# Context values times exponentials: two quarters in one product of 512 queries, at every second quarter of a neighbourhood-attention layer

## The chip, the cores and the metric

The kernel runs on one core of a Trainium2 chip. The metric is device time in microseconds (us) of one execution. Before the change the median of three runs is 630.89 us (629.98 to 631.63).

## The reference

One layer of a diffusion backbone: 1024 latent tokens on a grid of 16 x 64, 256 context tokens, 8 heads of 64. What matters here is the softmax that runs over a latent window and the whole context together:

```python
s_lat = jnp.einsum('biqhd,birkhd->bhiqrk', q_rot, k_rows) * scale + bias
s_lat = jnp.where(col_valid[:, None, :], s_lat, -jnp.inf)
s_ctx = jnp.einsum('biqhd,blhd->bhiql', q_plain, kc) * scale
p = jax.nn.softmax(jnp.concatenate([s_lat, s_ctx], axis=-1), axis=-1)
o = einsum('bhiqrk,birkhd->biqhd', p_lat, v_rows) + einsum('bhiql,blhd->biqhd', p_ctx, vc)
attn = o * jax.nn.silu(za)
conv = bg * conv3(cg * u) * jax.nn.silu(zc)
x_new = x + gate * (concatenate([attn, conv]) @ w_out)
```

Each of `q, k, v, za, u, bg, cg, zc` is a 512-column part of one input projection of the normalised, modulated tokens.

## The kernel before

All matrix products are made to float32 accuracy from parts in a rounded format: a tensor is split in a high part (a copy or an exponential by ScalarE, ACT in the rows) and the rest (a subtraction by VectorE, DVE). A product is then three matmuls on TensorE (PE): high x high, low x high, high x low. Names ending in `h` and `l` are these parts: `phc` and `plc` for the exponentials of the context, `phl` and `pll` for those of the latent window, `uh` and `ul` for projection weights.

The program has three stages. Up to some 275 us it normalises the tokens and projects q, k and v. From there to some 520 us it runs the attention, with the remaining projections (gates and convolution inputs) as filler between its matmuls. Then it makes the output projection.

The attention is a pipeline of 35 **quarters**, written out in order by `quarter(n)`; in this stage the order of every compute engine is fixed as written (`strict`), while the order of the DMA issues on SyncE (SP) is left to the scheduler. A quarter works on 256 queries (16 columns of the grid) of one head. In quarter n:

- the scores of unit n are made (`pss`, four matmuls), and the context scores of unit n+1 (`pc`, four matmuls; ScalarE copies half of it to `sc`);
- for unit e = n-2 the maximum per query is found: two transposes of the running maxima `mx` into `pmx`, called T in the prediction, a reduction `rm` on VectorE, and two transposes back (`back()`, `pmx<-ci,rm`) that spread the result over the partitions, copied by ScalarE to `mg`. VectorE then subtracts `mg` from `sc` and `sb`, and ScalarE takes the exponentials;
- unit o = n-3 is multiplied by V: `ctx_out` for the context (six matmuls of 65 output rows, 256 columns) and `lat_out` for the latent window, both added up in a bank of 512 queries, `po`.

VectorE's order in a quarter is: `rm`; `pll` of the unit before; up to three **chores** (work for the filler: splits `ul`, products of the convolution such as `cu<-pu,ub` and `cv<-pu,cv`); the subtractions of `mg`; the additions of the bias to `pss`, into `sb`; the maxima (`mx<-pc,sc`, then two `mx<-mx,sb`); `plc`. The next quarter's T reads `mx`.

The filler comes in **ticks** of six `pu` matmuls of 512 columns. `TICKS` gives each quarter's number, three in most, two in quarters 5 and 8, four in 17, 18, 27 and 28. A filler product of 24 matmuls fills one of two banks (tag `U`); the bank is free again when a copy or a chore has read it.

The lines of `quarter` that the change moves against each other are, in the order before:

```python
if live(o):
    heads[o // 4].ctx_out(o % 4)
do_dves(3)
if back and n > 2:
    back()
now = pair_of(n)
for i, hd_, j in now:
    hd_.scores(j, sbank[:, i])
for m in ctx_now:
    heads[m // 4].ctx_scores(m % 4)
if back and n == 2:
    back()
```

Of the kernel before, what the change touches and what calls it, by code (L numbers as in the profile page):

```python
# [19 lines left out]
P = 128  # L20
# [5 lines left out]
NB = 8  # L26
# [13 lines left out]
def body(tc, es, x, ctxt, w_ada, b_ada, w_in, q_g, k_g, rpbr, w_out, vecs, cst, out):  # L40
# [21 lines left out]
    pe, act, dve, pool = every = [ordered(e) for e in (nc.tensor, nc.scalar, nc.vector, nc.gpsimd)]  # L62
# [258 lines left out]
    def do_acts():  # L321
        for c in soon + (slow if not any(c[1] and c[1].__name__ == "product" for c in soon) else []):
            if c[0]:
                c[0]()
                c[0] = None

    def do_dves(most=99):
        while most > 0 and slow and slow[0][2] is not None and not slow[0][0]:
            slow.pop(0)[1]()
            most -= 1  # L330
        for queue in chores:
            while queue and not queue[0][0] and (queue is soon or most > 0 and not soon):
                on_dve = queue.pop(0)[1]
                if on_dve:
                    on_dve()
                    most -= 1
# [670 lines left out]
    class head:  # L1007
# [74 lines left out]
        def ctx_exp(self, g):  # L1082
            sc = self.cps[g]
            m = mg[:, g * 256:(g + 1) * 256].rearrange("p (o q) -> p o q", o=1)
            dve.tensor_tensor(sc, sc, m.broadcast_to([P, 2, 256]), ALU.subtract)
            ph = ap.tile([P, 2, 256], F32R, name="phc", tag="phc", bufs=1)
            pl = ap.tile([P, 2, 256], F32R, name="plc", tag="plc", bufs=1)
            act.activation(ph, sc, AF.Exp)
            act.activation(sc, sc, AF.Exp)
            self.cps[g] = ph, pl  # L1090
            return lambda: dve.tensor_tensor(pl, sc, ph[:].bitcast(F32), ALU.subtract)

        def ctx_out(self, g):
            ph, pl = self.cps.pop(g)
            for i in range(2):
                self.pv(g // 2, lambda o: o[:, (g % 2) * 256:(g % 2 + 1) * 256], NB + i, ph[:, i], pl[:, i], False)

        def finish(self, bank):

# [5 lines left out]
    def pair_of(n):  # L1105

        h, g = divmod(n, 4)
        return [(a, heads[h], 2 * g + a) for a in range(2)] if 0 <= h < NH else []

    def both(v, n, part=slice(0, 31)):  # L1110

        lo, hi = span(2 * (n % 4))
        return v[:, :, part.start * 12:min(part.stop, hi - lo) * 12]

    def maxima_of(n):

# [9 lines left out]
    def maxima(e):  # L1126

        blocks = turned(e) if e < 4 * NH else []
        nb = len(blocks)
        if not blocks:  # L1130
            return None
        pm = psm.tile([P, 512], F32, name="pmx", tag="C", bufs=2)
        for i, b in enumerate(blocks):
            pe.transpose(pm[:, i * P:(i + 1) * P], mx[:, b * P:(b + 1) * P], ident)
        rm = ap.tile([P, 2], F32, name="rm", tag="rm", bufs=8)
        dve.tensor_reduce(rm[:, :nb], pm[:, :nb * P].rearrange("p (i k) -> p i k", i=nb), AX.X, ALU.max)

        def back():
            for i in range(nb):
                pe.transpose(pm[:, 256 + i * P:256 + (i + 1) * P], rm[:, i:i + 1].broadcast_to([P, P]), ident)  # L1140
            v, step = mg[:, blocks[0] * P:], (blocks[-1] - blocks[0]) * P or P
            act.copy(bass.AP(v.tensor, v.offset, [list(v.ap)[0], [step, nb], [1, P]]),
                     pm[:, 256:256 + nb * P].rearrange("p (i k) -> p i k", i=nb))
        return back

    def quarter(n):

        live = lambda m: 0 <= m < 4 * NH
        ticks = TICKS[n]
        e, o = n - 2, n - 3
        back = maxima(e) if e >= 0 else None
        while lat_rest:
            lat_rest.pop()()
        if live(o):
            heads[o // 4].ctx_out(o % 4)
        do_dves(3)
        if gating and next(gating[0], "end"):  # L1160
            gating.pop(0)
        if back and n > 2:
            back()
        now = pair_of(n)
        for i, hd_, j in now:
            hd_.scores(j, sbank[:, i])
        if n == 0:
            next(fill)
            ticks -= 1
        ctx_now = [m for m in ([0, 1] if n == 0 else [n + 1]) if live(m)]  # L1170
        for m in ctx_now:
            heads[m // 4].ctx_scores(m % 4)
        if back and n == 2:
            back()
        if live(e):
            ctx_rest = heads[e // 4].ctx_exp(e % 4)
            sb = sbs.pop(e)
            w = both(sb, e)
            w4 = w.rearrange("p a (c r) -> p a c r", r=12)
            dve.tensor_tensor(w4, w4, maxima_of(e), ALU.subtract)  # L1180
            exps[e] = [ap.tile([P, 2, 384], F32R, name=m, tag=m, bufs=2) for m in ("phl", "pll")]
            ph, pl = (both(v, e) for v in exps[e])
            act.activation(ph, w, AF.Exp)
            act.activation(w, w, AF.Exp)
        for _ in range(n > 0):
            next(fill, None)
        done = []
        if o >= 0:
            pho, plo = exps.pop(o)
            for i, hd_, j in pair_of(o):  # L1190
                hd_.lat_out(j, pho[:, i], plo[:, i])
                if j in (5, 7):
                    done.append((hd_, j // 7))
                    if j == 7 and hd_.s:
                        ready.append(hd_.p)
        if now:
            sb = sbs[n] = sb_new()
            bt = now[0][1].bt[:].rearrange("p v n -> p (v n)")[:, :1128].rearrange("p (a n) -> p a n", a=2)
            for at, slot, w_ in (((0, 31, 8), (8, 15, 16)), ((0, 0, 31),), ((0, 0, 31),), ((0, 0, 15), (15, 39, 8)))[n % 4]:
                dve.tensor_tensor(sb[:, :, at * 12:(at + w_) * 12], sbank[:, :, at * 12:(at + w_) * 12],  # L1200
                                  bt[:, :, slot * 12:(slot + w_) * 12], ALU.add)
# [53 lines left out]
    for n in range(NT + 3):  # L1255
# [54 lines left out]
        if 1 < n <= NT + 1:  # L1310
            m, r = n - 2, (n - 2) % NB
# [69 lines left out]
    with sbuf("att") as ap, psum("psb") as psb:  # L1381
# [6 lines left out]
        for n in range(len(TICKS)):  # L1388
            h, g = divmod(n, 4)
            if 0 < h < NH and g == 0:  # L1390
                heads[h].load_v()
            if h + 1 < NH and g:
                nx = heads[h + 1]
                for load in ((nx.masks, nx.load_q), (nx.load_k,), ())[g - 1]:
                    load()
            quarter(n)
            if ready:
                p = ready.pop()
                if p < NPAIR - 1:
                    gating.append(gated(p))  # L1400
                else:
                    recip(p, ap)
# [146 lines left out]
```

## Time and profile before

| | before |
|---|---|
| median of three runs | 630.89 us (629.98 to 631.63) |
| the profiled execution | 630.4 us, of which the span of instructions is 628.6 us |
| TensorE busy | 621.7 us, 99% of the span |
| VectorE busy | 433.5 us, 69% |
| ScalarE busy | 326.5 us, 52% |
| granted TensorE clock | 0.999 of full speed |
| from 283.8 to 509.1 us | TensorE 225.13, VectorE 189.16, ScalarE 148.57 us busy of 225.30 |

A row of a timeline is: start in us, duration in us, engine, line, operation, output<-inputs, shapes, how many follow one another; in brackets the idle time of the engine before it and what ended that. Nearly all rows have line 55, since one helper records every operation, so that they are told apart by tile names. A row of the waits is: who waited, for whom, us in total, times, longest.

### The profile page before, as it was taken

The page shows a single profiled execution, that of the slowest core. Times are in us where ns is not written, and L with a number is a line of the kernel's source. Part 1 is how long each engine was busy: PE and PEld are TensorE (multiplying, and loading weights), DVE is VectorE, ACT ScalarE, POOL GpSimd, SP SyncE. Part 2 cuts the span into 40 slices and gives each one's busy share as a digit, 9 for nine tenths or more (in the row PEclk, how much of TensorE's full clock was granted, in tenths as well). Part 3 has the DMA queues.
Part 4 walks back from the last instruction along what each step waited for, and adds up shares of the span by engine and source line. Part 5 has one row for each costly group of instructions (what it writes and reads, how often), then busy time and mean ns, then how long its engine had stood idle before and what let it go on. Part 6 is the DMA issues. An engine that isn't in the chain of part 4 may idle for free.

```text
span 628.6 us, 10005 instructions
## 1 busy us (share of the span) xinstructions
PE 621.7 (99%) x3487; PEld 538.5 (86%) x3488; DVE 433.5 (69%) x889; ACT 326.5 (52%) x712; POOL 77.6 (12%) x102
## 2 busy tenths in 40 slices
PE   8999999999999999999999999999999999999998
PEld 3577899999999999888888888888888888888887
DVE  1887858866866855568897879988998865594111
ACT  3777835524625545346576568566774845450000
POOL 1305014113223221100000000000000002004200
PEclk9999999999999999999999999999999999999999
DMA  8983737967784995885474553775542235963621
GB/s 316 347 282 124 178 111 259 286 204 244 236 293 137 302 320 181 298 264 214 144 238 140 192 172 127 214 254 181 190 136 76 61 93 163 357 226 121 213 102 50
DMA packets 104030, 126.45 MB, mean 201 GB/s; under 512 B 10689, under 2 KB 70553, under 8 KB 102700
## 3 DMA queue, kind: packets, MB, share of 16 engines
q1 hardware_dynamic: 97516, 114.24, 55.3%
q10 hardware_dynamic: 6208, 11.05, 5.6%
q0 software_dynamic: 256, 0.54, 0.3%
q8 instruction: 27, 0.44, 0.3%
q14 instruction: 23, 0.19, 0.1%
HBM read 89.04 MB, written 39.04 MB: 204 GB/s over the span
## 4 chain that ended last, share of the span: by engine, by line
PE 96%; DMA 2%; SPq 1%; ACT 0%; issue 0%; DVE 0%; ACTq 0%
PE pu L55 29%; PE pacc L55 21%; PE po L55 8%; PE acc L55 6%; PE pout L75 5%; PE pout L74 5%; PE pout L76 5%; PE tr L55 4%; PE cacc L55 4%; PE pss L55 3%; PE pc L55 2%; PE pmx L55 2%; DMA xx<-in_x 2%; PE trA L55 1%; PE trB L55 1%; SPq L55 1%
## 5 line engine op out<-in xcount | busy, mean ns | idle before, releaser
L55 PE MATMUL pu<-h,uh 128*128 128x512 f32 x544 | 170.0, 394 | 0.0
L55 PE MATMUL pacc<-w,h 128*128 128x384 f32 x768 | 138.4, 337 | 0.0
L55 PEld LDWEIGHTS pacc<-w,h 128*128 128x128 f32 x768 | 132.7, 188 | 0.2
L55 PEld LDWEIGHTS pu<-h,uh 128*128 128x128 f32 x544 | 97.6, 188 | 16.8 <-ACT zs L55 0.2
L55 PE MATMUL pu<-h,ul 128*128 128x512 f32 x272 | 106.6, 392 | 0.0
L55 PEld LDWEIGHTS pu<-h,ul 128*128 128x128 f32 x272 | 51.1, 188 | 11.2
L55 POOL TENSOR_TENSOR ss<-ss,few 128x4 f32<-128x4 f32 (+1 forms) x40 | 41.9, 1049 | 124.8 <-DVE ss L55 124.8
L75 PE MATMUL pout<-wol,yh 128*128 128x512 f32 (+2 forms) x136 | 51.6, 379 | 0.0
L74 PE MATMUL pout<-woh,yh 128*128 128x512 f32 (+2 forms) x136 | 51.5, 379 | 0.0
L76 PE MATMUL pout<-woh,yl 128*128 128x512 f32 (+2 forms) x136 | 50.8, 379 | 0.0
L55 PE MATMUL acc<-h,w 128*128 128x512 f32 x144 | 38.1, 404 | 0.8 <-ACT h L55 0.8
L55 ACT ACTIVATE sq<-pacc 128x256 f32<-128x256 f32 x32 | 12.4, 388 | 47.5 <-PE pacc L55 43.7
L55 DVE TENSOR_REDUCE rm<-pmx 128x2 f32<-128x256 f32 (+1 forms) x33 | 13.8, 417 | 32.7 <-PE pmx L55 32.6
L55 ACT COPY mg<-pmx 128x256 f32<-128x256 f32 (+1 forms) x33 | 12.1, 366 | 46.4 <-PE pmx L55 42.0
L55 DVE TENSOR_TENSOR mx<-mx,sb 128x372 f32<-128x372 f32 (+2 forms) x64 | 31.9, 498 | 1.9
L55 PE MATMUL po<-phl,v 128*65 128x276 f32 (+2 forms) x192 | 32.0, 269 | 0.0
L55 DVE TENSOR_REDUCE ss<-sq 128x4 f32<-128x260 f32 (+1 forms) x40 | 15.7, 392 | 23.6 <-ACT sq L55 23.6
L55 ACT ACTIVATE qn<-pacc,ss 128x64 f32<-128x64 f32 x128 | 30.2, 333 | 3.0 <-POOL ss L55 3.0
L55 PEld LDWEIGHTS acc<-h,w 128*128 128x128 f32 x144 | 25.5, 188 | 6.5 <-ACT h L55 1.2
L1479 DVE TENSOR_TENSOR ot<-pout,xr 128x512 f32<-128x512 f32 (+2 forms) x9 | 5.7, 632 | 35.4 <-PE pout L76 33.3
L55 ACT COPY sc<-pc 128x512 f32<-128x512 f32 x32 | 18.8, 589 | 21.1 <-PE pc L55 21.0
L74 PEld LDWEIGHTS pout<-woh,yh 128*128 128x128 f32 x136 | 25.6, 188 | 4.7
(159 smaller groups left out, 1194.4 us busy)
## 6 DMA issues: line engine op xcount, KB each, us to landing
uraw<-in_w_in SPq DMA_DIRECT2D x34, 256.0 KB
q_d<-qs SPq DMA_DIRECT2D x32, 256.0 KB
k_s<-k_d SPq DMA_DIRECT2D x8, 1024.0 KB
q_s<-q_d SPq DMA_DIRECT2D x16, 512.0 KB
wr<-in_w_in SPq DMA_DIRECT2D x40, 192.0 KB
slab<-in_w_ada SPq DMA_DIRECT2D x6, 1024.0 KB
v_d<-vs SPq DMA_DIRECT2D x20, 260.0 KB
v<-v_d SPq DMA_DIRECT2D x16, 325.0 KB
```

Of the source, the lines that this page charges most:

```text
L55: i = emit(*a, **kw)
L74: i = pe.matmul(ps, ah, bh, start=first, stop=False)
L75: pe.matmul(ps, ah, bl, start=False, stop=False)
L76: pe.matmul(ps, al, bh, start=False, stop=last)
L1479: dve.tensor_tensor(ot[:, c], ps[c.start][:, c], xr[:, c], ALU.add)
```

## The change

The exponentials of the context of two units, an even one and the odd one behind it, are put side by side in one tile of 512 columns per part. `ctx_out` does nothing for an even unit; for an odd one it multiplies V by both at once, six matmuls of 512 columns into the whole bank. Where o is even (quarters 3, 5, ... 33), the transposes back come behind the scores and context scores; where o is odd (4, 6, ... 34) they come behind the six wide matmuls. To make room, `pll` has one buffer in place of two.

```diff
-            ph = ap.tile([P, 2, 256], F32R, name="phc", tag="phc", bufs=1)
-            pl = ap.tile([P, 2, 256], F32R, name="plc", tag="plc", bufs=1)
+            if g % 2 == 0:
+                self.cx = [ap.tile([P, 2, 512], F32R, name=name, tag=name, bufs=1) for name in ("phc", "plc")]
+            ph, pl = (v[:, :, g % 2 * 256:g % 2 * 256 + 256] for v in self.cx)
             act.activation(ph, sc, AF.Exp)
             act.activation(sc, sc, AF.Exp)
...
         def ctx_out(self, g):
-            ph, pl = self.cps.pop(g)
-            for i in range(2):
-                self.pv(g // 2, lambda o: o[:, (g % 2) * 256:(g % 2 + 1) * 256], NB + i, ph[:, i], pl[:, i], False)
+            if g % 2:
+                ph, pl = self.cx
+                for i in range(2):
+                    self.pv(g // 2, lambda o: o, NB + i, ph[:, i], pl[:, i], False)
...
-        if back and n > 2:
+        early = live(o) and o % 2
+        if back and early:
             back()
...
-        if back and n == 2:
+        if back and not early:
             back()
...
-            exps[e] = [ap.tile([P, 2, 384], F32R, name=m, tag=m, bufs=2) for m in ("phl", "pll")]
+            exps[e] = [ap.tile([P, 2, 384], F32R, name=m, tag=m, bufs=b) for m, b in (("phl", 2), ("pll", 1))]
```

On TensorE, quarter 5 (o = 2, even), from the last filler matmul of quarter 4 on:

```order
 L55 MATMUL pu<-h_227,ul 128x512
 L55 MATMUL pmx<-ci,mx 128x128 x2
-L55 MATMUL po<-phc,v_3314 65x256 x2
-L55 MATMUL po<-plc,v_3314 65x256
-L55 MATMUL po<-phc,v_3314 65x256 x2
-L55 MATMUL po<-plc,v_3314 65x256
-L55 MATMUL pmx<-ci,rm 128x128 x2
 L55 MATMUL pss<-q_s,k_s 128x372 x4
 L55 MATMUL pc<-q_s,kc_s 128x256 x4
+L55 MATMUL pmx<-ci,rm 128x128 x2
 L55 MATMUL pu<-h_228,uh 128x512 x2
```

The six context matmuls are gone, and the transposes back stand behind `pss` and `pc`. The quarter after it on TensorE, quarter 6 (o = 3, odd):

```order
 L55 MATMUL pmx<-ci,mx 128x128 x2
-L55 MATMUL po<-phc,v_3314 65x256 x2
-L55 MATMUL po<-plc,v_3314 65x256
-L55 MATMUL po<-phc,v_3314 65x256 x2
-L55 MATMUL po<-plc,v_3314 65x256
+L55 MATMUL po<-phc,v_3314 65x512 x2
+L55 MATMUL po<-plc,v_3314 65x512
+L55 MATMUL po<-phc,v_3314 65x512 x2
+L55 MATMUL po<-plc,v_3314 65x512
 L55 MATMUL pmx<-ci,rm 128x128 x2
```

Here the order stays and the six are twice as wide. On ScalarE, from the end of quarter 4 into quarter 5, before:

```order
L55 CAST uh<-uraw 128x512
L55 COPY mg<-pmx 128x2x128
L55 COPY sc<-pc 128x512
L55 ACTIVATE phc<-sc 128x512
L55 ACTIVATE sc<-sc 128x512
L55 ACTIVATE phl<-sb 128x2x276
```

and with the change:

```order
L55 CAST uh<-uraw 128x512
L55 COPY sc<-pc 128x512
L55 COPY mg<-pmx 128x2x128
L55 ACTIVATE phc<-sc 128x2x256
L55 ACTIVATE sc<-sc 128x512
L55 ACTIVATE phl<-sb 128x2x276
```

The copy of the maxima has changed places with the copy of the context scores, as in all quarters 3, 5, ... 31. VectorE's instructions and their order are the same in both; `plc` writes two runs of 256 in place of one of 512. On SyncE, some loads of `uraw` have moved behind the loads of `q_s` and `k_s`.

More of the change, by code (lines that the diff above doesn't have):

```diff
@@ L1085, in ctx_exp @@
             dve.tensor_tensor(sc, sc, m.broadcast_to([P, 2, 256]), ALU.subtract)
-            ph = ap.tile([P, 2, 256], F32R, name="phc", tag="phc", bufs=1)
-            pl = ap.tile([P, 2, 256], F32R, name="plc", tag="plc", bufs=1)
+            if g % 2 == 0:
+                self.cx = [ap.tile([P, 2, 512], F32R, name=name, tag=name, bufs=1) for name in ("phc", "plc")]
+            ph, pl = (v[:, :, g % 2 * 256:g % 2 * 256 + 256] for v in self.cx)
             act.activation(ph, sc, AF.Exp)
             act.activation(sc, sc, AF.Exp)
-            self.cps[g] = ph, pl
-            return lambda: dve.tensor_tensor(pl, sc, ph[:].bitcast(F32), ALU.subtract)
+            del self.cps[g]
+            return lambda: dve.tensor_tensor(pl, sc, ph.bitcast(F32), ALU.subtract)
         def ctx_out(self, g):
-            ph, pl = self.cps.pop(g)
-            for i in range(2):
-                self.pv(g // 2, lambda o: o[:, (g % 2) * 256:(g % 2 + 1) * 256], NB + i, ph[:, i], pl[:, i], False)
+            if g % 2:
+                ph, pl = self.cx
+                for i in range(2):
+                    self.pv(g // 2, lambda o: o, NB + i, ph[:, i], pl[:, i], False)
         def finish(self, bank):
```

## The prediction

> **What bounds the kernel now.** I read the page first, then the waits of VectorE over the attention part, then the timelines of TensorE, VectorE and ScalarE quarter by quarter. A quarter's clock starts at its first transposes `pmx<-ci,mx`, called T below.
>
> ```profile
> PE 621.7 (99%) x3487; PEld 538.5 (86%) x3488; DVE 433.5 (69%) x889; ACT 326.5 (52%) x712; POOL 77.6 (12%) x102
> PE 96%; DMA 2%; SPq 1%; ACT 0%; issue 0%; DVE 0%; ACTq 0%
> ```
>
> TensorE is the bound: 96% of the chain that ended last is TensorE work, so time removed from it shows in the result, and so does any new wait of it. A matmul's end is modelled, so its cost is read from start to start, here in quarter 19 (T at 401.49):
>
> ```profile
> 400.58 0.39 PE L55 MATMUL pu<-h,ul 128*128 128x512 f32 x1
> 400.81 0.61 PE L55 MATMUL pu<-h,uh 128*128 128x512 f32 x2
> 401.26 0.39 PE L55 MATMUL pu<-h,ul 128*128 128x512 f32 x1
> 401.49 0.38 PE L55 MATMUL pmx<-ci,mx 128*128 128x128 f32 x2
> 401.62 0.48 PE L55 MATMUL po<-phc,v 128*65 128x256 f32 x2
> 401.94 0.28 PE L55 MATMUL po<-plc,v 128*65 128x256 f32 x1
> 402.06 0.40 PE L55 MATMUL po<-phc,v 128*65 128x256 f32 x2
> 402.29 0.28 PE L55 MATMUL po<-plc,v 128*65 128x256 f32 x1
> 402.41 0.41 PE L55 MATMUL pmx<-ci,rm 128*128 128x128 f32 x2
> ```
>
> Four products of 512 go from 400.58 to 401.49: 0.228 us each. Four context products of 256 go from 401.94 to 402.41: 0.118 us each. So 512 columns cost 1.93 times 256; the rows' second column (0.39 and 0.28 us) would mislead.
>
> What TensorE can be made to wait for stands on VectorE:
>
> ```profile
> DVE rm L55 <- PE pmx L55: 32.6, 28, 3.9
> ```
>
> The reduction `rm` is VectorE's first work that needs a new quarter's T. In 28 quarters VectorE had finished the quarter before and stood waiting, 32.6 us in all, some 1.2 us each. That is the room by which TensorE now leads the race, and it is not even.
>
> **The change, part by part.** *Products.* 192 of 256 columns go: 192 x 0.118 = 22.7 us. 96 of 512 come: 96 x 0.228 = 21.9 us. Gain 0.8 us. The 512 price is that of `pu`, whose stationary operand is 128 wide and not 65; I take it, since the streamed columns are the same. Bounds: 0.236 (twice the short product, no gain at all) and, far below, a weight-load pace treated as a rival. [...]
>
> *The cover of the reduction.* Six products now lie between T and the transposes back. They end at 402.41, where the reduction's result has only just come (the row below, 401.91 + 0.42 = 402.33), and the pair of transposes back then runs some 0.03 us late. Afterwards six products of 512 (1.37 us), or scores and context scores (1.2 us), lie there: 30 x 0.03 = 0.9 us gained. In two or three quarters whose T came directly behind VectorE, the third context product waits some 0.1 us more for `plc`; that goes too, 0.2 us. TensorE's own work so shrinks by 0.8 + 0.9 + 0.2, about 1.8 us.
>
> *The evenness.* The work leaves one quarter and comes back in the next. An odd quarter (3, 5, ... 33: sixteen) loses 6 x 0.118 + 0.03 = 0.73 us, an even one (4, 6, ... 34) gains 6 x 0.228 - 6 x 0.118 - 0.03 = 0.63 us. VectorE's instructions and their order stay. So an odd quarter is 0.73 us shorter on TensorE alone, and where VectorE or a buffer holds TensorE there, the 0.73 is lost while the 0.63 in the next is still paid. This is the term that decides, so each odd quarter is priced.
>
> First, banks of the filler. In quarter 19 the filler `pu` behind the scores needs a bank that `cv<-pu,cv` must first read:
>
> ```profile
> 401.91 0.42 DVE L55 TENSOR_REDUCE rm<-pmx 128x2 f32<-128x256 f32 x1 [0.18 <-PE pmx L55]
> 402.91 0.69 DVE L55 TENSOR_TENSOR cv<-pu,cv 128x512 f32<-128x512 f32 x1
> 403.65 0.50 PE L55 MATMUL pu<-h,uh 128*128 128x512 f32 x1
> ...
> 479.71 0.68 DVE L55 TENSOR_TENSOR cv<-pu,cv 128x512 f32<-128x512 f32 x1
> 480.45 0.50 PE L55 MATMUL pu<-h,uh 128*128 128x512 f32 x1
> ```
>
> `cv` ends at 403.60 and 480.39 and `pu` starts 0.05 and 0.06 us later. `cv` stands behind `rm` on VectorE and so comes at the same time after T as before. TensorE, 0.73 us earlier, waits for it: quarters 19 and 29 lose all of it, 2 x 0.73.
>
> Second, the copy of the maxima. With scores first, ScalarE's queue has `sc<-pc` ahead of `mg<-pmx`. Quarter 2 has this very order in the trace of before:
>
> ```profile
> 277.53 0.38 PE L55 MATMUL pmx<-ci,mx 128*128 128x128 f32 x2
> 278.91 0.38 PE L55 MATMUL pmx<-ci,rm 128*128 128x128 f32 x2
> 279.11 0.59 ACT L55 COPY sc<-pc 128x512 f32<-128x512 f32 x1
> 279.59 0.38 ACT L55 COPY mg<-pmx 128x256 f32<-128x256 f32 x1
> 280.00 0.69 DVE L55 TENSOR_TENSOR sc<-sc,mg 128x512 f32<-128x512 f32 x1 [0.76 <-ACT mg L55]
> ```
>
> VectorE's subtraction starts 2.47 us after T. Queued behind it are all of that quarter's scores and maxima, and behind those TensorE's next T. [...] If `mg` could go first, it would start at most 0.48 us earlier (279.11), quarter 5 below would lose no less than 0.32 us instead of 0.80, and the sum would be 2.0 at the least.
>
> ```profile
> 298.50 0.28 PE L55 MATMUL pmx<-ci,mx 128*128 128x128 f32 x1
> 300.47 0.69 DVE L55 TENSOR_TENSOR sc<-sc,mg 128x512 f32<-128x512 f32 x1
> 303.59 0.55 DVE L55 TENSOR_TENSOR mx<-mx,sb 128x372 f32<-128x372 f32 x1
> 304.71 0.27 PE L55 MATMUL pmx<-ci,mx 128*128 128x128 f32 x1
> ```
>
> Quarter 5 has only two ticks of filler. Its subtraction starts 1.97 after T, afterwards 2.47; its last maximum ends at 5.64, afterwards 6.14; TensorE would want the next T at 6.21 - 0.73 = 5.48 and gets it no earlier than 6.14 + 0.14 = 6.28 (0.14 is the least distance seen, quarter 31 below). It loses 0.80.
>
> Third, the maxima themselves. In the other tight quarters chores keep VectorE busy past 2.47, so nothing moves on it and only the room counts, last maximum's end to next T:
>
> ```profile
> 451.58 1.12 DVE L55 TENSOR_TENSOR mx<-mx,sb 128x372 f32<-128x372 f32 x2
> 453.15 0.27 PE L55 MATMUL pmx<-ci,mx 128*128 128x128 f32 x1
> ...
> 467.82 0.91 DVE L55 TENSOR_TENSOR mx<-mx,sb 128x276 f32<-128x276 f32 x2
> 469.25 0.27 PE L55 MATMUL pmx<-ci,mx 128*128 128x128 f32 x1
> ...
> 498.78 0.93 DVE L55 TENSOR_TENSOR mx<-mx,sb 128x276 f32<-128x276 f32 x2
> 499.85 0.30 PE L55 MATMUL pmx<-ci,mx 128*128 128x128 f32 x1
> ```
>
> Quarter 25 has 0.45 us, 0.14 of it needed: 0.31 can be won, 0.42 is lost. Quarter 27 has 0.52: 0.35 lost. Quarter 31 has 0.14 and is held by VectorE already: all 0.73 lost.
>
> Fourth, quarter 33 has no scores, so nothing covers its reduction:
>
> ```profile
> 509.12 0.27 PE L55 MATMUL pmx<-ci,mx 128*128 128x128 f32 x1
> 509.43 0.29 DVE L55 TENSOR_REDUCE rm<-pmx 128x1 f32<-128x128 f32 x1 [3.88 <-PE pmx L55]
> 509.93 0.27 PE L55 MATMUL pmx<-ci,rm 128*128 128x128 f32 x1
> ```
>
> The transposes back move from 0.81 to about 0.66 after T (0.60 plus 0.06 of hand-over): 0.15 won, 0.58 lost.
>
> The other nine odd quarters keep their gain: the room in the first of them, quarter 3, and in the tightest, quarter 23, is
>
> ```profile
> 288.85 0.45 DVE L55 TENSOR_TENSOR mx<-mx,sb 128x276 f32<-128x276 f32 x1
> 291.00 0.27 PE L55 MATMUL pmx<-ci,mx 128*128 128x128 f32 x1
> ...
> 436.17 0.92 DVE L55 TENSOR_TENSOR mx<-mx,sb 128x276 f32<-128x276 f32 x2
> 438.03 0.27 PE L55 MATMUL pmx<-ci,mx 128*128 128x128 f32 x1
> ```
>
> 1.70 and 0.94 us; 0.94 - 0.73 leaves 0.21, just over 0.14. In 3, 7, 9 and 15 the subtraction also comes later by 0.3 to 0.7; their room is about that of quarter 3 or more. In even quarters the longer TensorE covers the later `mg` (six products of 0.228 push the transposes back by 0.63, and T by the same).
>
> *At nothing:* one buffer for `pll` instead of two, since `pll` is written behind the next T and its reader stands ahead of that T on TensorE (in quarters 4 and 7, where it is written in the quarter itself, the reader is two microseconds earlier); the strided `plc` and `phc` halves, as many elements in the same instruction; on SyncE's queue two loads of `q_s` and `k_s` now pass `uraw`, which is needed a whole unit of eight ticks later. If that cover failed, a quarter would wait about one issue, 0.6 us at most. TensorE's order behind the attention part is unchanged and it is the bound there, so the shift goes through to the end.
>
> *Sum.* Lost: 1.46 + 0.80 + 0.42 + 0.35 + 0.73 + 0.58 = 4.34 us. Against 1.8 gained: 2.5 us slower. The profiled execution took 630.4 us, 0.5 below the median 630.89 of the runs shown; with the change 632.9 there, 633.4 as a median.
>
> **The rivals.** *No wait appears* (faster): only TensorE's 1.8 us count, 629.1 us. For it: 32.6 us of room. Against it: the room is uneven and three of the seven priced places stand at 0.05 to 0.14 us. It decides if `cv` in quarters 19 and 29 and the maxima in 25 to 31 come 0.7 us earlier after T than before, for which no instruction moves. Chance 0.06. *The two bank waits are absorbed* because the filler's first product can be issued and only its result held: 4.34 - 1.46 - 1.8 = 1.1 us slower, 632.0, within the bound; other single terms missing give the like. Chance 0.32. *Every odd quarter gives its 0.73 back* because VectorE becomes the bound in all of them: 16 x 0.63 - 0.2 is 9.9 us, 640.8. It decides where the room is under 0.87 in all sixteen; nine rooms speak against it. Chance 0.05. *The 65-wide products run at the weight loads' pace* of some 0.14 us apart instead of 0.228: 96 x 0.09 = 8.6 us of work less, 625 to 627. The weight loads of `pu` are longer and still the rows show 0.228. [...] Chance 0.02. That the change does not do what it says is excluded by the instruction orders shown above.
>
> **How the numbers follow.** The forecast, 2.5 us with terms that can miss by some 1.5, has 0.55. A measurement tells 0.3% from no change, 1.9 us. Slower by more: 0.55 and 0.05, of which a little goes to the bound's inside, 0.58. Same: 0.34. Faster: 0.08. The range reaches down to 630.3, with half of the losses missing, and up to 637, with the nine loose quarters losing a third of their 0.73 each.
>
> **What would show it.** Right: 96 products of 512 at 0.23 us; VectorE's wait before `rm` gone behind quarters 25, 27 and 31 and larger behind every even one; `pu` right behind `cv` in 19 and 29; the subtraction 2.4 us after T in quarters 3 to 9; quarter 5 no shorter than before. Wrong: odd quarters all 0.73 shorter (faster), or T behind the last maximum by 0.14 in most of them (10 us), or 512-column products well under 0.2 us.

## The result, and the profile after

| | before | after |
|---|---|---|
| median of six runs | 630.45 us (629.98 to 631.63) | 633.16 us (632.55 to 634.05) |
| ratio after to before | | 1.0041, 95% interval 1.0028 to 1.0054 |
| the profiled execution | 630.4 us, span 628.6 us | 632.55 us, span 630.8 us |

The change makes the kernel 0.4% slower, 2.7 us of the medians; 633.4 us was forecast, with a chance of 0.58 for slower.

The page after, its busy times and the engines of the chain that ended last:

```profile
PE 621.7 (99%) x3392; PEld 530.2 (84%) x3392; DVE 434.0 (69%) x889; ACT 326.0 (52%) x712; POOL 77.8 (12%) x102
PE 91%; DVE 4%; ACT 3%; issue 1%; POOL 0%; ACTq 0%; DVEq 0%; POOLq 0%
```

TensorE's matmuls fell by 95 in the records (96 by the program; a few records are missing) and its busy time not at all (that time is modelled). What is new is in the second line: VectorE and ScalarE hold 7% of the chain, where they held nothing. TensorE now waits for them at places. The longer span is found by the starts of TensorE's work at four marks: first product of the q, k and v projection, first T, last T (quarter 33), first product of the output projection. TensorE's timeline of before, then of after, start and duration in us:

```profile
77.69 0.52 PE L55 MATMUL pacc<-w,h 128*128 128x384 f32 x2
274.58 0.27 PE L55 MATMUL pmx<-ci,mx 128*128 128x128 f32 x1
537.23 0.39 PE L74 MATMUL pout<-woh,yh 128*128 128x512 f32 x1
```

```profile
76.62 0.51 PE L55 MATMUL pacc<-w,h 128*128 128x384 f32 x2
273.49 0.27 PE L55 MATMUL pmx<-ci,mx 128*128 128x128 f32 x1
510.68 0.27 PE L55 MATMUL pmx<-ci,mx 128*128 128x128 f32 x1
539.37 0.39 PE L74 MATMUL pout<-woh,yh 128*128 128x512 f32 x1
```

From the first T to the last it is 234.54 us before (509.12 - 274.58) and 237.19 after: 2.65 longer. From the last T to the output projection it is 28.11 and 28.69: 0.58 longer. So the changed part of the program costs 3.2 us in this execution. The first T came 1.1 us earlier here, and was so already at the first mark, 76.62 against 77.69. The compute engines' orders are the same up to there, so this start is not the change's; it hides a third of the cost in the span. In the profiled executions of all twelve kernels of this document the first mark lies between 76.0 and 77.7 us, and the first T follows it by 196.9 us in each. Kernels are therefore compared below by these stages as well as by their medians.

The lengths of the quarters, T to T, show the form of it. The nine odd quarters that were forecast to keep their gain (3, 7, 9 to 17 and 21, 23) are 0.65 to 0.80 us shorter, 0.72 in the mean (0.73 forecast). The fifteen even ones, 4 to 32, are 0.59 to 0.68 longer, 0.65 in the mean (0.63 forecast). The priced ones:

| quarter | before | after | change | forecast |
|---|---|---|---|---|
| 5 | 6.21 | 6.28 | +0.07 | +0.07 |
| 19 | 7.20 | 7.18 | -0.02 | 0 |
| 25 | 7.64 | 7.33 | -0.31 | -0.31 |
| 27 | 8.81 | 8.41 | -0.40 | -0.38 |
| 29 | 7.70 | 7.71 | +0.01 | 0 |
| 31 | 6.83 | 6.84 | +0.01 | 0 |

Each of these has its row in the trace after. Quarter 5, T at 297.26, on all three engines:

```profile
297.26 0.27 PE L55 MATMUL pmx<-ci,mx 128*128 128x128 f32 x1
298.83 0.58 ACT L55 COPY sc<-pc 128x512 f32<-128x512 f32 x1 [1.81 <-PE pc L55]
299.32 0.38 ACT L55 COPY mg<-pmx 128x256 f32<-128x256 f32 x1
299.73 0.69 DVE L55 TENSOR_TENSOR sc<-sc,mg 128x512 f32<-128x512 f32 x1 [0.42 <-ACT mg L55]
302.85 0.55 DVE L55 TENSOR_TENSOR mx<-mx,sb 128x372 f32<-128x372 f32 x1
303.54 0.30 PE L55 MATMUL pmx<-ci,mx 128*128 128x128 f32 x1 [0.58 <-ACT ob L55]
```

`sc` goes ahead of `mg` on ScalarE, the subtraction starts 2.47 us after T as it did in quarter 2 of before, the last maximum ends at 303.40, and T follows 0.14 later. TensorE stood idle for 0.58 us before it. The row names `ob` as the releaser, which had long been done; it is the maximum that came last.

Quarters 19 and 29, the filler bank:

```profile
402.04 0.69 DVE L55 TENSOR_TENSOR cv<-pu,cv 128x512 f32<-128x512 f32 x1
402.78 0.50 PE L55 MATMUL pu<-h,uh 128*128 128x512 f32 x1 [0.58 <-DVE cv L55]
...
480.04 0.68 DVE L55 TENSOR_TENSOR cv<-pu,cv 128x512 f32<-128x512 f32 x1
480.77 0.50 PE L55 MATMUL pu<-h,uh 128*128 128x512 f32 x1 [0.59 <-DVE cv L55]
```

`pu` starts 0.05 us after `cv` ends, as before, but now a wait of 0.6 stands in its row. Quarters 25, 27 and 31, the last maximum and the next T:

```profile
451.31 1.12 DVE L55 TENSOR_TENSOR mx<-mx,sb 128x372 f32<-128x372 f32 x2
452.58 0.30 PE L55 MATMUL pmx<-ci,mx 128*128 128x128 f32 x1 [0.28 <-ACT ob L55]
...
467.84 0.91 DVE L55 TENSOR_TENSOR mx<-mx,sb 128x276 f32<-128x276 f32 x2
468.90 0.30 PE L55 MATMUL pmx<-ci,mx 128*128 128x128 f32 x1
...
499.74 0.93 DVE L55 TENSOR_TENSOR mx<-mx,sb 128x276 f32<-128x276 f32 x2
500.82 0.31 PE L55 MATMUL pmx<-ci,mx 128*128 128x128 f32 x1 [0.60 <-DVE mx L55]
```

The distances from the maximum's end to T are 0.15, 0.15 and 0.15 us: all three stand behind VectorE, where 25 and 27 had 0.45 and 0.52 before. And in quarter 33 the transposes back stand 0.66 us after T, with a wait for the reduction that did not exist before:

```profile
511.34 0.32 PE L55 MATMUL pmx<-ci,rm 128*128 128x128 f32 x1 [0.39 <-DVE rm L55]
```

The price of a wide product is read in quarter 6, first product to the transposes back:

```profile
303.71 0.71 PE L55 MATMUL po<-phc,v 128*65 128x512 f32 x2
304.25 0.40 PE L55 MATMUL po<-plc,v 128*65 128x512 f32 x1
304.49 0.62 PE L55 MATMUL po<-phc,v 128*65 128x512 f32 x2
304.95 0.39 PE L55 MATMUL po<-plc,v 128*65 128x512 f32 x1
305.17 0.38 PE L55 MATMUL pmx<-ci,rm 128*128 128x128 f32 x2
```

From 304.25 to 305.17 there are four products: 0.23 us each, although the stationary operand is 65 wide. The forecast took 0.228 from `pu`.

The waits of VectorE from 278 to 522 us (total, times, longest) have changed in two lines; the second of before is shown first, then both of after:

```profile
DVE sc L55 <- ACT mg L55: 2.0, 5, 0.8
```

```profile
DVE rm L55 <- PE pmx L55: 26.1, 23, 4.5
DVE sc L55 <- ACT mg L55: 8.4, 13, 0.9
```

VectorE waits less for a new T (32.6 us in 28 quarters before), and more for the copy of the maxima. In the even quarters the transposes back come some 0.6 us later; in seven of them (4, 6, 10, 12, 14, 22 and 30) VectorE waits for that copy, 5.2 us of the 8.4, and that is where its lead over TensorE goes there.

### The profile page after: what moved, and what is told of

It reads as the page before. It is cut to its first block, busy times and chain, and to the rows that moved or that the text cites. A ratio compares the mean times of both kernels' runs of the same rounds, so it can differ in the third digit from the quotient of the medians.

```text
span 630.8 us, 9829 instructions
## 1 busy us (share of the span) xinstructions
PE 621.7 (99%) x3392; PEld 530.2 (84%) x3392; DVE 434.0 (69%) x889; ACT 326.0 (52%) x712; POOL 77.8 (12%) x102
## 4 chain that ended last, share of the span: by engine, by line
PE 91%; DVE 4%; ACT 3%; issue 1%; POOL 0%; ACTq 0%; DVEq 0%; POOLq 0%
PE pu L55 26%; PE pacc L55 21%; PE po L55 7%; PE acc L55 6%; PE pout L75 5%; PE pout L76 5%; PE pout L74 5%; PE tr L55 5%; PE cacc L55 4%; PE pss L55 2%; PE pmx L55 2%; PE pc L55 2%; PE trA L55 1%; PE trB L55 1%; DVE sc L55 1%
## 5 line engine op out<-in xcount | busy, mean ns | idle before, releaser
L55 PE MATMUL pu<-h,uh 128*128 128x512 f32 x544 | 171.3, 396 | 1.4 <-DVE cv L55 1.2
L55 PE MATMUL pacc<-w,h 128*128 128x384 f32 x768 | 138.4, 337 | 0.0
L55 PEld LDWEIGHTS pacc<-w,h 128*128 128x128 f32 x768 | 132.7, 188 | 0.2
L55 PEld LDWEIGHTS pu<-h,uh 128*128 128x128 f32 x544 | 97.6, 188 | 18.9 <-DVE cv L55 1.7
L55 PE MATMUL pu<-h,ul 128*128 128x512 f32 x272 | 106.6, 392 | 0.0
L55 PEld LDWEIGHTS pu<-h,ul 128*128 128x128 f32 x272 | 51.1, 188 | 11.3
L55 POOL TENSOR_TENSOR ss<-ss,few 128x4 f32<-128x4 f32 (+1 forms) x40 | 41.9, 1049 | 124.8 <-DVE ss L55 124.8
L74 PE MATMUL pout<-woh,yh 128*128 128x512 f32 (+2 forms) x136 | 51.5, 379 | 0.0
L55 PE MATMUL acc<-h,w 128*128 128x512 f32 x144 | 38.1, 405 | 0.8 <-ACT h L55 0.8
L55 ACT COPY sc<-pc 128x512 f32<-128x512 f32 x32 | 18.7, 588 | 36.4 <-PE pc L55 31.2
L55 ACT ACTIVATE sq<-pacc 128x256 f32<-128x256 f32 x32 | 12.4, 387 | 48.0 <-PE pacc L55 47.5
L55 DVE TENSOR_REDUCE rm<-pmx 128x2 f32<-128x256 f32 (+1 forms) x33 | 13.7, 416 | 28.5 <-PE pmx L55 28.3
L55 DVE TENSOR_TENSOR mx<-mx,sb 128x372 f32<-128x372 f32 (+2 forms) x64 | 31.9, 498 | 2.0
L55 PE MATMUL po<-phl,v 128*65 128x276 f32 (+2 forms) x192 | 32.0, 269 | 0.0
L55 ACT ACTIVATE phc<-sc 128x512 fp32r<-128x512 f32 x32 | 20.3, 634 | 22.6 <-DVE sc L55 22.5
L55 DVE TENSOR_REDUCE ss<-sq 128x4 f32<-128x260 f32 (+1 forms) x40 | 15.7, 392 | 23.3 <-ACT sq L55 23.3
L55 ACT ACTIVATE qn<-pacc,ss 128x64 f32<-128x64 f32 x128 | 30.1, 333 | 3.0 <-POOL ss L55 3.0
L55 PEld LDWEIGHTS acc<-h,w 128*128 128x128 f32 x144 | 25.5, 188 | 6.5 <-ACT h L55 1.2
L74 PEld LDWEIGHTS pout<-woh,yh 128*128 128x128 f32 x136 | 25.6, 188 | 4.7
```

The source lines that it names most:

```text
L55: i = emit(*a, **kw)
L74: i = pe.matmul(ps, ah, bh, start=first, stop=False)
```

## Experiments

The theory of the prediction, A in the expectations, is unevenness: work that leaves an odd quarter is lost where VectorE or a bank holds TensorE there, and is paid for in full in the even one. The rivals B and C, as the expectations state them, put the cost elsewhere: in the order of scores and transposes back itself, or in what the wide product costs. In the tables below "T to T" is the stage from the first T to that of quarter 33, "last" from there to the first product of the output projection, "output" from there to the end of the span.

| kernel | median us | ratio to before | T to T | last | output |
|---|---|---|---|---|---|
| before | 630.45 | | 234.54 | 28.11 | 91.4 |
| after | 633.16 | 1.0041 (1.0028 to 1.0054) | 237.19 | 28.69 | 91.4 |
| narrow products in the new places | 633.58 | 1.0055 (1.0042 to 1.0068) | 237.51 | 28.73 | 91.5 |
| new order, narrow products in each quarter | 631.27 | 1.0020 (1.0007 to 1.0033) | 234.50 | 28.74 | 95.4 |
| half a tick moved | 631.62 | 1.0026 (1.0013 to 1.0040) | 235.36 | 28.68 | 92.9 |
| latent products ahead of the tick as well | 629.14 | 0.9990 (0.9981 to 0.9998) | 233.40 | 28.59 | 91.9 |
| the same, quarter 33 covered | 629.34 | 0.9989 (0.9978 to 1.0000) | 233.47 | 28.08 | 92.8 |
| the same, three loads later | 628.66 | 0.9981 (0.9969 to 0.9993) | 233.42 | 28.09 | 91.4 |
| before, `pll` on GpSimd | 632.12 | 1.0024 (1.0006 to 1.0042) | 236.47 | 28.12 | 91.4 |
| after, `pll` on GpSimd | 634.89 | 1.0069 (1.0057 to 1.0082) | 238.95 | 28.68 | 91.5 |
| before, a maximum done three times | 640.71 | 1.0169 (1.0152 to 1.0185) | 245.43 | 28.12 | 91.4 |
| after, a maximum done three times | 647.77 | 1.0278 (1.0262 to 1.0295) | 251.99 | 28.67 | 91.4 |

Ratios are to the kernel before on the same chip; its median there was between 629.89 and 630.45 us.

### Narrow products in the wide ones' places

Both quarters' context products stay together in the even quarter, but each of 512 is made as two of 256.

```diff
-                    self.pv(g // 2, lambda o: o, NB + i, ph[:, i], pl[:, i], False)
+                    for half in range(2):
+                        cols = slice(half * 256, half * 256 + 256)
+                        self.pv(g // 2, lambda o: o[:, cols], NB + i, ph[:, i, cols], pl[:, i, cols], False)
```

> The changed kernel, but each product of 512 queries is made as two of 256 in the same place, so the even quarters do all twelve. Theory A (the work is uneven: odd quarters are held by VectorE or a bank, even ones pay in full): width matters little, TensorE gets 16 x (12 x 0.118 - 6 x 0.228) = 0.8 us more work, 633.9 us. Rival C (a product of 512 into a whole bank is what costs): back to about the kernel before, 630.5 us.

It is not faster than the change: 1.0055 against 1.0041, T to T 237.51 against 237.19. The wide products are not the cost, and rival C is out. Their gain is small; quarter 6 of TensorE's timeline has the narrow ones, ten of them from 304.69 to 305.86:

```profile
304.69 0.28 PE L55 MATMUL po<-plc,v 128*65 128x256 f32 x1
...
305.86 0.38 PE L55 MATMUL pmx<-ci,rm 128*128 128x128 f32 x2
```

0.117 us each, 0.234 for two against 0.23 for a wide one. Twelve against six then make some 0.02 to 0.05 us in an even quarter, which is what T to T shows (0.3 in all). The forecast gain of 0.8 us lies above that; the medians differ by 0.0014 of 630 us, 0.9 us, but their intervals overlap.

### The new order of the odd quarters, without the move

The kernel before, with scores, context scores, transposes back and then the six narrow context products in each odd quarter. The order around the scores is the changed kernel's there, and no work leaves the quarter.

```diff
+        early = live(o) and o % 2
-        if live(o):
+        if live(o) and early:
             heads[o // 4].ctx_out(o % 4)
...
-        if back and n > 2:
+        if back and early:
             back()
...
-        if back and n == 2:
+        if back and not early:
             back()
+        if live(o) and not early:
+            heads[o // 4].ctx_out(o % 4)
```

> The kernel before, with narrow products in every quarter, but in the odd quarters 3 to 33 the transposes back come behind the scores and context scores, and the context products behind them. Theory A: lengths stay even, so only quarter 33 (0.55 us, its reduction uncovered) and quarter 5 (0 to 0.1 us) lose, the covered reductions win 0.4: 630.2 to 631.0 us. Rival B (the later copy of the maxima is what costs): most of the 2.7 us, 632.5 to 633.2 us.

T to T is 234.50 us, as before (234.54): over the whole attention the new order by itself costs nothing. Quarter 5 is 6.28 us long, 0.07 more, and quarter 32 0.32 more; against that stand quiet odd quarters (7, 9, 11, 13, 15, 21 and 23) that are 0.02 to 0.05 shorter each, since their reduction is now covered. Quarter 33, which has no scores, gives the 0.63 more in "last". The kernel is 1.4 us slower by the medians, of which "last" explains 0.6. The profiled execution took 634.20 us, the longest of this kernel's twelve, and what it lost besides lies in the output projection, in one wait of TensorE's weight loads:

```profile
PEld pout L74 <- ACT yh L1456: 2.2, 1, 2.2
```

What follows that wait is dealt with in the last section. The other executions have no trace, so the remaining 0.8 us of the median stay unexplained. The verdict on the attention rests on the stage, not on the median.

### Half a tick moved from even to odd quarters

If unevenness is the cost, then evening out TensorE's quarters should give it back. The changed kernel, with three of the filler's products (0.68 us) moved from each even quarter to the odd one, at the quarter's end; ticks are counted in halves.

```diff
-        ticks = TICKS[n]
+        ticks = 2 * TICKS[n] + (n % 2 * 2 - 1 if n > 2 else 0)
...
-        for _ in range(ticks - (n > 0)):
-            next(fill, None)
+        tick(ticks)
```

> The changed kernel with half a tick of filler (three products of 512, 0.68 us) moved from each even quarter to the odd one before it, at the quarter's end. Theory A: quarters are even again, 0.04 us shorter than before each; the losses in 25, 27, 31 go, the bank waits of 19 and 29 (1.4 us) and quarter 33 (0.6 us) stay: 630.0 to 631.2 us. Rival B or C: the moved filler changes nothing, 633 us.

T to T falls from 237.19 to 235.36. All quarters are back within 0.15 us of their lengths before (5 at 6.28, 25 at 7.58, 31 at 6.98), but for two: 19 and 29 are 0.67 and 0.69 longer than before, because TensorE still reaches `pu` as early as in the changed kernel, and the wait stands at the bank. The waits of the weight loads, 278 to 522 us:

```profile
PEld pu L55 <- DVE cv L55: 1.7, 2, 0.8
```

The changed kernel has the same row word for word. So the bank waits belong to what lies between T and `pu`, and what lies at the quarter's end does not reach them. The output projection lost 1.5 us in the profiled execution, again to `yh` (`PEld pout L74 <- ACT yh L1464: 1.4, 1, 1.4`). That execution took 631.87 us, near the median of 631.62, which lies 0.4 above the expected values.

### Latent products ahead of the tick

To put cover back between T and `pu` in the odd quarters, `lat_out` goes ahead of the first tick there. In quarter 33 the half tick also goes between T and the transposes back.

```diff
+        swap = live(o) and o % 2 == 0
-        if n > 0:
+        if n > 0 and not swap:
             tick(2)
             ticks -= 2
...
+        if swap:
+            tick(2)
+            ticks -= 2
```

> As the one with the moved half tick, and in odd quarters the latent products stand ahead of the first tick of filler, which then starts some 1.3 us later, behind the read of its bank; in quarter 33 half a tick stands between the transposes and those back. Theory A: the bank waits and quarter 33's loss go too, 628.4 to 629.3 us, faster than both kernels. Rival B or C: 632 to 633 us.

The row of waits for `cv` is gone; quarters 19 and 29 are 7.06 and 7.58 us long, below their 7.20 and 7.70 before. T to T is 233.40, 1.1 us under the kernel before. Not all of it need be the wide products' gain: 0.59 of it stands in quarters 19, 27 and 29 (0.33 in 27), where the filler, and with it the need of a bank, now comes later. The median, 629.14 us, is in theory A's range and far from the rivals' 632 to 633; it is 0.8 us under the kernel before on that chip. Quarter 33 didn't gain, against what A expected, because `lat_out`, now early, waited for `pll` there (`PEld po L55 <- DVE pll L55: 0.7, 2, 0.4` over two places).

### Quarter 33 covered by the half tick alone

As before this, but without the swap in quarter 33 (`and now` added to `swap`), so that three filler products lie between T and the transposes back and `lat_out` stays late.

> As the kernel with the latent products first, but in quarter 33, where these waited 0.5 us for the rest of the exponentials, a tick of filler stands ahead of them again. Theory A: 0.5 us less than that kernel up to the output projection, 1.3 us less than the kernel before; as the output projection then starts earlier against its loads, which keep the DMA engines full, some of it can be given back there: 0.5 to 1.3 us under the kernel before.

"Last" is 28.08 us, as in the kernel before (28.11) and 0.6 less than with the change: the uncovered reduction was the cost there. The median, 0.9 us under the kernel before on that chip, is within the range expected, but its ratio is that of the kernel without this cover (0.9989 and 0.9990). In the profiled execution the output projection lost the time, with a wait of 1.3 us for `yh` (`PEld pout L74 <- ACT yh L1471: 1.3, 1, 1.3`).

### Less work on VectorE

If VectorE's share in the odd quarters is what holds TensorE, then moving `pll` (0.83 us a quarter) from VectorE to GpSimd should shrink the cost of the change. Both kernels were run with it.

```diff
-            lat_rest.append(lambda: dve.tensor_tensor(pl, w, ph.bitcast(F32), ALU.subtract))
-            if n + 1 >= len(TICKS) or TICKS[n + 1] == 2:
-                lat_rest.pop()()
+            pool.tensor_tensor(pl, w, ph.bitcast(F32), ALU.subtract)
```

> The kernel before, with the rest of the latent exponentials (pll) computed on GpSimd in place of VectorE, so that VectorE has 0.75 to 0.93 us more room in each quarter. Both theories: no slower than the kernel before unless GpSimd and VectorE hold each other up; 629 to 632 us. It is the base for the next run.

> The changed kernel with pll on GpSimd, to be compared with the run before it. Theory A: with the room larger the losses of quarters 25, 27 and 31 (1.5 us) and the bank waits of 19 and 29 (1.5 us, their read comes 0.75 to 0.93 us sooner) go; quarter 5 (0.8) and quarter 33 (0.6) stay; the change then costs nothing or wins up to 0.5 us, in place of costing 2.7. Rival B (the later copy of the maxima): VectorE's room does not change when that copy comes, the change still costs 2 to 3 us.

The total missed: theory A expected no cost, and the change costs 634.89 - 632.12 = 2.8 us here too. The base is itself 1.9 us slower than the kernel before, just above its expected range. But the places of the cost moved. Quarters 25 and 29 became 0.75 and 0.73 us shorter by the change, as theory A has it for a VectorE with room, and 19 and 27 1.02 and 1.33 shorter, some of which is only that the base is longer there (by 0.34 and 0.24). Quarters 5 and 31 won nothing; for 31 A had expected the gain. The loss is new, in six even quarters (6, 10, 14, 22, 26, 30) that are 1.0 to 1.7 longer in place of 0.65. There TensorE waits for `plc`, as it does in four quarters of the base (3, 19, 26 and 27, 3.0 us in all). The waits of the weight loads with the change, from 278 to 522 us, then the operations of VectorE with `pll` on GpSimd, before and after the change (busy, mean ns), and a place of it in the second kernel:

```profile
PEld po L55 <- DVE plc L55: 5.2, 6, 1.3
```

```profile
L55 DVE TENSOR_TENSOR plc<-sc,phc 128x512 fp32r<-128x512 f32 x32 | 26.8, 837 | 1.2 <-ACT sc L55 1.2
```

```profile
L55 DVE TENSOR_TENSOR plc<-sc,phc 128x512 fp32r<-128x512 f32 x32 | 32.7, 1021 | 1.2 <-ACT sc L55 1.2
...
332.13 1.49 POOL L55 TENSOR_TENSOR pll<-sb,phl 128x552 fp32r<-128x552 f32 x1 [4.05 <-ACT sb L55]
332.30 1.86 DVE L55 TENSOR_TENSOR plc<-sc,phc 128x512 fp32r<-128x512 f32 x1
...
334.22 0.44 PE L55 MATMUL po<-plc,v 128*65 128x512 f32 x1 [0.22 <-DVE plc L55]
```

`plc` takes 0.68 us when alone and 1.86 when it starts behind `pll`: GpSimd ends at 333.62 and `plc` at 334.16. The wide products read it right behind T, so the even quarter waits. This experiment changed two things at once, VectorE's room and the length of `plc`, and its total decides nothing between the theories; the lengths of 25 and 29 speak for A, that of 31 does not.

### More work on VectorE

The other way round: the second maximum of `sb` is made three times in each quarter, in both kernels (64 more of 0.50 us, 1 us more for VectorE in each). Theory A then expects a dearer change, since more odd quarters have no room.

```diff
+        for _ in range(2):
+            hd_.lat_max(j, sb[:, i])
```

> The kernel before, with the second of each quarter's two maxima (mx<-mx,sb) done three times over, which changes no value and costs VectorE 0.92 to 1.13 us more ahead of each next T. From the rooms in the trace of before, what exceeds them adds up to some 9 us: 639 us, 637 to 641. It is the base for the next run.

> The changed kernel with the same extra work on VectorE. Theory A (uneven quarters spend VectorE's room): its odd quarters have 0.7 us less room, so the same extra work adds some 12 to 13 us, and the change now costs 5 to 7.5 us against the run before it. Rivals B and C (the later copy, or the wide products themselves): a cost that does not depend on VectorE's room, so the change still costs 2.7 us, 2 to 3.5.

The change costs 647.77 - 640.71 = 7.1 us, within what A expects and over twice what the rivals do. (The extra work by itself cost more than expected in both: 10.8 us in the kernel before, where some 9 were expected, and some 15 in the changed one, where 12 to 13 were.) Quarters 21 and 22 show how, by their T. TensorE's timeline of the kernel before with this work:

```profile
421.79 0.41 PE L55 MATMUL pmx<-ci,mx 128*128 128x128 f32 x2
429.59 0.41 PE L55 MATMUL pmx<-ci,mx 128*128 128x128 f32 x2
436.88 0.38 PE L55 MATMUL pmx<-ci,mx 128*128 128x128 f32 x2
```

And of the changed kernel with this work:

```profile
425.19 0.38 PE L55 MATMUL pmx<-ci,mx 128*128 128x128 f32 x2
432.97 0.41 PE L55 MATMUL pmx<-ci,mx 128*128 128x128 f32 x2 [0.78 <-DVE mx L55]
440.86 0.38 PE L55 MATMUL pmx<-ci,mx 128*128 128x128 f32 x2
```

Quarter 21 lasts 7.80 and 7.78 us, where it gave 0.65 in the change alone, and TensorE waits 0.78 us for the maximum at its end. Quarter 22 lasts 7.29 and 7.89. The 0.6 is paid and nothing is won for it: the rival of the prediction in which the odd quarters give all back, made to happen.

The later copy of the maxima has no part in most of this. In nine odd quarters, 11, 13, 19, 21, 23, 25, 27, 29 and 31, VectorE's subtraction starts at the same distance from T in both kernels (to 0.02 us), and yet none of them is more than 0.02 us shorter. These nine alone lose 9 x 0.72 = 6.5 us that they would have won. In 3, 5, 7, 9 and 15 the subtraction does come later, by 0.27 to 0.63 us, and quarter 5 is 0.50 longer for it; so the copy's price does depend on VectorE's room, against what the expectation says of rival B. That the cost is 7 us and not 10 has two reasons: five odd quarters (3, 7, 9, 15 and 17) still gained 0.2 to 0.3, and three even ones (16, 18 and 26), behind which TensorE waits for VectorE with the same work in the kernel before too, are at most 0.03 longer.

### A version that keeps the gain

The kernel with quarter 33 covered left one loss, the output projection's wait for `yh`. In that stage ScalarE waits for its loads `tb` (2.11 us ahead of the `yh` at 527.00, for one). From 515 to 556 us 14 loads `tb` of `y` and the first three loads `xr` of the residual were issued, and the DMA share is 0.99 to 1.05 from 530 to 550. Here the first three of these wait until the last `y` but one is split, by a copy of one column.

```diff
         xr = rp.tile([P, 512], F32, name="xr", tag="xr", bufs=3)
+        if not nh and t < 3:
+            act.copy(xr[:, 0:1], y[3][1][:, 0:1].bitcast(F32))
         sp.dma_start(xr, x[0, rows, cols])
```

> The kernel with balanced quarters and quarter 33 covered, and in the output projection the first three loads of x (0.77 MB) wait until the last attention head's input is ready, so that they don't share the full DMA engines with the inputs that TensorE waits for. If the gain is given back there by the full DMA engines: 0.5 to 1.4 us less than the same kernel without this, 1.5 to 2.0 us under the kernel before. If those waits have another cause: no difference.

The waits between 505 and 640 us are gone altogether, and the output projection takes 91.4 us as in both kernels. 628.66 us, 0.9981 of before (0.9969 to 0.9993), is 1.3 us less than the kernel before on that chip, under the 1.5 to 2.0 expected, and 0.6% less than the change as it was made (0.9981 / 1.0041 is 0.9940). Against the kernel without the later loads (0.9989) the times alone show no difference, since the intervals overlap; that the wait is gone is shown by the trace. The waits of TensorE's weight loads in the attention, 276 to 520 us, name no bank any more:

```profile
PEld pmx L55 <- issue: 0.9, 3, 0.3
PEld pmx L55 <- ACT sb L55: 0.8, 1, 0.8
PEld pmx L55 <- ACT ob L55: 0.4, 1, 0.4
PEld po L55 <- DVE pll L55: 0.3, 1, 0.3
PEld pmx L55 <- DVE rm L55: 0.2, 1, 0.2
```

Short waits for VectorE remain: behind quarters 5, 8, 27 and 31 T follows the last maximum by 0.14 or 0.15 us, after a wait of some 0.3 us that the rows put down to `ob` and to "issue". All the balanced kernels also have the one buffer for `pll`, so that this buffer costs nothing that can be seen.

So wide products are worth a little when TensorE's quarters stay as even as they were, and cost when they don't.

## Why the prediction was right

The mechanism and the places were right. The size came out near, 2.7 us against 2.5, and that is in part luck: the profiled executions put the cost of the changed part at 3.2. By its own steps:

- *The evenness.* Odd quarters 0.72 shorter (0.73 forecast), even ones 0.65 longer (0.63). That the loss goes with the room of VectorE and of the banks is shown: with room taken away the change costs 7.1 us, with three filler products and the latent products moved it costs nothing, and narrow products in the new places cost the same. The one attempt to give VectorE more room failed in its total, since the means brought a new wait.
- *The banks.* All of it lost in 19 and 29, as forecast. The rival in which they absorb it (0.32) did not happen: the wait stands at the first product of `pu`, in its own row.
- *The copy of the maxima.* Quarter 5 is 6.28 us long, the number forecast, with the subtraction 2.47 after T. With the new order alone, and no work moved, quarter 5 is 6.28 us long as well, so that this end is set by the copy; over the whole attention the new order costs nothing.
- *The maxima.* 25, 27 and 31 to within 0.02 us. Quarter 23, which was forecast to keep its gain with 0.21 us of room, did so, with 0.24 left.
- *Quarter 33.* Transposes back at 0.66 after T, the number forecast.
- *TensorE's own gain, 1.8 us.* This term was over-sized. A pair of quarters without trouble gains 0.72 - 0.65 = 0.07 us, some 1.1 over sixteen pairs, and the version without the new waits gains 1.1 in T to T, though 0.59 of that stands in quarters 19, 27 and 29, as said. The products give 0.3 and not 0.8 when measured with narrow ones in the same place. The rival of the weight loads' pace did not come: in the changed kernel the loads of 65 columns take 0.136 us and those of `pu` 0.189, while wide products are 0.23 us apart. The covered reductions are borne out at 0.02 to 0.05 a quarter (0.03 forecast), and the 0.2 for `plc` was not measured by itself. So the attention grew by 3.2 us and not by 2.5. The median's 2.7 lies between. The 1.1 us of an earlier start in the profiled execution belong to that execution: the engines' orders do not differ up to there.
- *What would show it.* One sign failed. VectorE's wait before `rm` shrank behind most odd quarters, but did not grow behind every even one by what TensorE came later: behind quarters 4, 6 and 10, for example, it was 1.12, 1.45 and 1.56 before and 1.11, 1.56 and 1.59 after. What VectorE won there it spent waiting for `mg` in the even quarter, as in four others. The other signs came: behind 25, 27 and 31 there is no wait, and in quarters 3 to 9 the subtraction starts 2.29 to 2.47 us after T.
- *The range.* Its ends, 630.3 and 637, are wider than the words beside them: half of the losses missing gives 631.3, and a third of the loose quarters' gain lost gives 635.6.

In sum: the six quarters of the table measure -0.64 us together, where 6 x 0.73 = 4.38 would have been won without waits, so 3.74 are lost there. With the 0.58 forecast for quarter 33, whose own length no later T marks, it is 4.3 us, as forecast. Against that stand 1.1 us gained in place of 1.8, which makes the 3.2.

## What to carry to other kernels

When work moves between neighbouring stages of a pipeline, TensorE's total says little (here its own work in the attention shrank by some 1.1 us, and the attention grew by 3.2): price each stage that gets shorter by the room of the engine or buffer that ends it, and count the stage that gets longer in full. A merger that saves TensorE time pays in full only if other work, a filler with no due time, goes the opposite way, and to the right place: between the same two waits from which the work was taken, not merely into the same stage. And time won ahead of a later stage can be lost again in that stage, as in the wait of 1.3 us for `yh` in the kernel with quarter 33 covered, so look there before counting it.

## What the runs showed of the hardware

*VectorE and GpSimd held each other up.* With `pll` on GpSimd, `plc` on VectorE (512 columns) has two durations and nothing between in the changed kernel's attention: 0.68 to 0.69 us in 23 records and 1.86 to 1.92 in nine. A long one starts while `pll` runs and ends about 0.55 us after it. So it is from 332.30 to 334.16, behind a `pll` that ends at 333.62. A `plc` that starts ahead of `pll` keeps its 0.68 or 0.69 us, and `pll` can be the longer one then: 744 columns took 2.10 us from 478.22, 0.22 behind the start of a `plc`, and 1.79 from 509.68, where VectorE was idle.

*The granted clock fell after a wait of 2.2 us.* In the profiled execution of the kernel with the new order alone, TensorE's matmuls after the wait for `yh`:

```profile
555.35 0.50 PE L74 MATMUL pout<-woh,yh 128*128 128x512 f32 x1 [1.82 <-ACT yh L1456]
...
556.54 0.63 PE L74 MATMUL pout<-woh,yh 128*128 128x512 f32 x1
556.96 0.63 PE L75 MATMUL pout<-wol,yh 128*128 128x512 f32 x1
```

They start 0.42 or 0.43 us apart from 556.54 to 559.52, against 0.23 before the wait. The granted clock is 0.76 from 553 to 560 us (the third column from the end), and 1.00 from 545 to 553 and from 560 to 570:

```profile
553.00:560.00 7.00, 5.18 (x15) 3.50 (x14) 5.47 (x10) 3.07 (x7) 0.00 (x0) 0.76 0.84 254
```

So 2.2 us of waiting cost some 4 us of "output" (95.4 against 91.4): at 0.23 us a product, 2.0 were lost from 553.14 to 555.35, and as much again in the eleven steps from there to 559.82. One execution shows it, and the slow stretch lasted some 3.4 us (556.07 to 559.52). In the kernel with quarter 33 covered the products behind the wait of 1.3 us are 0.23 us apart again from 553.38 on, 1.1 us after the first of them. In the kernel with half a tick moved, with its wait of 1.4 us, the mean granted clock of the profiled execution was 0.999, against 0.996 in the one above.

*In the output projection an earlier start was often lost again.* The kernels whose TensorE reached it at 537.23 us (before) or later waited there 0.3 us at most; the four without later loads that reached it earlier, from 534.97 to 537.21, waited 0.8 to 2.6 us for `yh` and `yl`. In that stretch the DMA engines are full, as in this window of the kernel with quarter 33 covered (granted clock, DMA share and GB/s are the last three columns):

```profile
545.00:550.00 5.00, 5.00 (x24) 4.14 (x23) 1.74 (x3) 2.28 (x4) 0.00 (x0) 1.00 1.05 403
```

That the loads `xr` crowd out those of `y` is inferred from the last kernel alone, where their delay took the wait away although it arrived earliest, at 534.41. The time of arrival does not decide it by itself: at 537.21 us TensorE waited 1.8 us, at 537.23 not at all, and at 536.05 only 0.8. What else does stays open.
